# In the first block's mixers, ten of 25 input tiles and all twelve output tiles stay whole float32 and are multiplied in two passes; the other tiles are split as before

## The chip, the cores and the metric

The kernel runs on one core of a Trainium2 chip. A core has five engines that run side by side, each through its own list of instructions in order: TensorE (PE in the profile, its weight loads PEld), VectorE (DVE), ScalarE (ACT), GpSimd (POOL) and SyncE (SP), whose queue here issues nearly all loads from the chip's memory. The engines wait for one another by semaphores. The metric is the device time of one execution in microseconds (us).

## The reference

Two transformer-like blocks work one after the other on a sequence of 256 tokens of width 1024, in float32. Each block is a pair of token mixers followed by an expert layer (PEER) that scores 16,384 small experts. The change lies in the first block's mixers alone:

```
mod = (silu(c) @ w_ada + b_ada)              # six vectors of 1024: shifts, scales, gates
h = rmsnorm(x, norm_mix) * (1 + scale_m) + shift_m
proj = h @ w_in                              # 1024 -> 3088 columns
y_pool = pool_mixer(proj[:, :512])           # trailing means of 2, 4, 8, 16 tokens, then 128x128 per group
y_ssd = ssd_mixer(z, xbc, dt)                # causal convolution, SiLU, chunked state space, gate, rmsnorm
y = concat(y_pool, y_ssd) @ w_out            # 1536 -> 1024
x = x + gate_m * y
```

## The kernel before, in words

Everything is held transposed: a tile has 128 channels on the partitions and the 256 tokens in the free dimension. A weight tile is 128 by 8 by 128 float32 values (512 KB): the eight 128x128 blocks that make 128 output channels from 1024 inputs. The whole kernel consumes 645 such tiles in one fixed list (`self.items`), filled by `plan` and walked by `fetch_to` (L72: issue the load on SP), `high` (L79: ScalarE writes `whi`, the tile rounded to the matmul's reduced float32r type, L90), `low` (L93: VectorE writes `wlo = raw - whi`, L97) and `take` (L107), which prepares tiles two ahead of the product that it is called for and issues loads three tiles beyond that. `raw`, `whi` and `wlo` have three buffers each.

The activations are split in the same way into `hh` and `hl`. A product (`product_steps`, L119) then makes, for each of eight k, three float32r matmuls of 256 columns: `whi` by `hh` (L124), `whi` by `hl` (L125), `wlo` by `hh` (L126). Products land in PSUM buffers `mm`, of which there are three.

Nothing is scheduled by a planner: each engine's instructions stand in the order in which the Python code emits them. The first block's mixers (`mixer1`) run in this order:

- **The start** (L384 to L468). Sixteen rows of `w_ada` are reduced against `silu(c)` (`ada`, L306: a multiply with a running sum, L313 on VectorE; the first three on GpSimd and ScalarE). Along the way come the modulation (`g`, `mod`: L417, L418), the activations `h[k]` (ScalarE, for k of 6 and 7 VectorE, L426), `hh`, `hl` (`rest`, L431) and the products of the first two input tiles (`pair`), which run together, five of eight k inside the loop and three behind it.
- **The input tiles** (L716 on). 25 tiles in the order of `M1`: time steps, four tiles of B and C, eight of x, eight of z, four for pooling. After each product comes its evacuation (`evac`): a four-tap convolution (L357 on ScalarE, then three L359 on VectorE) and SiLU for the x, B and C tiles, a gate for z, sums over windows for pooling (L644 to L653). The list `steps` and the numbers in this loop place the state-space work beside it (`decays`, `outputs`), and from n = 5 on one `ada` row per tile. Work that has to wait a tile goes through the list `post`.
- **The outputs** (L745 on). Each output y is split into `yh` (ScalarE, L629, L665) and `yl` (VectorE, L630, L666). Eight tiles `w_outs` (1024 state-space channels) and four `w_outp` (512 pooling channels for two output tiles each; `both`, L752) follow: a pair, then in turns `out(f + 2)`, `residual(f)` and `both`. `residual` (L762) adds to x and prepares the next layer's split input `gh`, `gl`.
- **What follows.** The expert layer's first two products take `gh` and `gl` while the last residuals are made; then comes its norm, and the rest of the kernel, with 608 split tiles.

Of the kernel before, what the change touches and what calls it, by code (L numbers as in the profile page):

```python
# [18 lines left out]
T = 256  # L19
D = 1024  # L20
KT = 8
# [30 lines left out]
class Net:  # L52
# [16 lines left out]
    def plan(self, key, index, eng=None, spare=False):  # L69
        self.items.append([key, index, eng, None, spare])  # L70

    def fetch_to(self, n):  # L72
        while self.fetched < min(n, len(self.items)):
            it = self.items[self.fetched]
            it[3] = self.stream.tile([128, KT, 128], F32, name="raw", bufs=RAW)
            self.nc.sync.dma_start(it[3], self.a[it[0]][it[1]])
            self.fetched += 1

    def high(self, n):  # L79
# [4 lines left out]
        self.fetch_to(n + 1)  # L84
        if it[4]:
# [33 lines left out]
    def product_steps(self, ps, key, index, xh, xl, clear=True, prep=PREP):  # L119

        nc = self.nc
        hi, lo = self.take(key, index, prep)
# [11 lines left out]
    def proj(self, key, index, xh, xl):  # L134
# [229 lines left out]

    def plan_mixer1(self):
        for n, i in enumerate(self.M1):
            self.plan("w_in", i, eng=None)
        for f in range(0, 8, 2):
            self.plan("w_outs", f)
            self.plan("w_outs", f + 1)  # L370
            self.plan("w_outp", f // 2)

    def mixer1(self, constants):
        tc, nc, a = self.tc, self.nc, self.a
        with self.sbuf("m1") as m1, self.sbuf("w1", 2) as wk, self.psum("q1", 3) as self.pp, self.psum("p1", 3) as px:
            xs = m1.tile([128, 8, T], F32, name="xs")
            self.scratch_in(m1)
# [4 lines left out]
            with self.sbuf("early") as self.ap:  # L382
# [30 lines left out]
                h = {}  # L413

                def scaled(k):
# [4 lines left out]
                    h[k] = self.ap.tile([128, T], F32, name="nt4", bufs=4)  # L420
                    if k < 6:
                        nc.scalar.activation(self.hh[:, k], xs[:, k], AF.Identity, scale=g[:, k:k + 1],
                                             bias=m[:, k:k + 1])
                        nc.scalar.activation(h[k], xs[:, k], AF.Identity, scale=g[:, k:k + 1], bias=m[:, k:k + 1])
                    else:
                        nc.vector.tensor_scalar(h[k], xs[:, k], g[:, k:k + 1], m[:, k:k + 1], op0=ALU.mult,  # L426
                                                op1=ALU.add)
                        nc.scalar.copy(self.hh[:, k], h[k])

                def rest(k):  # L430
                    nc.vector.tensor_sub(self.hl[:, k], h.pop(k), self.hh[:, k].bitcast(F32))  # L431
# [3 lines left out]
                rests = {4: (0, 1), 5: (2, 3), 6: (4, 5), 7: (6, 7)}  # L435
# [1142 lines left out]
```

## Time and profile before

| | |
|---|---|
| median of 3 runs | 2187.42 us (2176.32 to 2188.99) |
| profiled execution | 2172.73 us, of which the span that the profile shows is 2170.9 us |
| first block's mixers in that span | 0 to about 199 us |
| busy over the span | TensorE 92%, VectorE 73%, ScalarE 51%, GpSimd 2% |
| load of one tile, from issue to landing | 3.2 to 4.6 us, median by kind |

In the profile, a row of the timeline has the start and the duration in us, the engine, the line of the program, the operation and its operands (out<-in); in brackets stands how long the engine had been idle and what ended that. The ends of matmuls are modelled and pipelined: one of 256 columns shows 0.28 us where the next starts 0.11 us after it, so TensorE's pace is read from starts, not from durations. The same holds, less so, for VectorE and ScalarE, whose next instruction starts a little before the end of the last.

### The profile page before, as it was taken

How to read it: one execution, taken by the hardware profiler on the slowest of the kernel's cores; microseconds unless marked ns; L12 is line 12 of the kernel's file. 1: busy time of each engine (PE TensorE's matmuls, PEld its weight loads, DVE VectorE, ACT ScalarE, POOL GpSimd, SP SyncE). 2: the span in 40 equal slices, each digit the busy share in tenths (PEclk: the TensorE clock that was granted, in tenths of full speed). 3: DMA queues.
4: the chain of work that ended last, by engine and by line, in shares of the span. 5: the costliest groups of instructions: out<-in, count | busy, mean ns of one | idle time of the engine just before them, and what ended most of it. 6: DMA issues, size and time to landing. Idle time of an engine off the chain costs nothing.

```text
span 2170.9 us, 41970 instructions
## 1 busy us (share of the span) xinstructions
PE 1987.4 (92%) x16976; PEld 1947.6 (90%) x16976; DVE 1581.9 (73%) x3061; ACT 1107.3 (51%) x1965; POOL 53.2 (2%) x52
## 2 busy tenths in 40 slices
PE   5888888877999999999999998987789999999998
PEld 4778888777999999999999998887779999999998
DVE  7998899788655556765688779998885555555555
ACT  4564444555544445444576554446554444444444
POOL 3021000000000000000000010000000000000000
PEclk9999999999999999999999999999999999999999
DMA  7755344322555555755545564443236555555553
GB/s 256 253 183 189 141 155 142 116 94 100 195 191 187 192 193 195 258 199 185 188 154 175 185 223 137 151 151 107 89 107 208 190 187 192 193 187 189 189 185 128
DMA packets 102723, 376.67 MB, mean 174 GB/s; under 512 B 11648, under 2 KB 12032, under 8 KB 101504
## 3 DMA queue, kind: packets, MB, share of 16 engines
q1 hardware_dynamic: 101520, 369.38, 49.1%
q0 software_dynamic: 576, 4.19, 0.5%
q8 instruction: 133, 2.18, 0.4%
q14 instruction: 62, 0.51, 0.1%
q10 hardware_dynamic: 432, 0.41, 0.1%
HBM read 370.80 MB, written 3.15 MB: 172 GB/s over the span
## 4 chain that ended last, share of the span: by engine, by line
PE 62%; DVE 27%; ACT 6%; issue 3%; DMA 1%; SPq 0%; DVEq 0%; ACTq 0%
PE acc L1341 11%; PE acc L1340 11%; PE acc L1342 11%; PE mm L126 9%; PE mm L125 9%; PE mm L124 9%; DVE wlo L97 8%; ACT whi L90 3%; DVE og L1236 2%; DVE aw L313 2%; DVE oh L1231 1%; DVE I L959 1%; DVE rep L965 1%; DVE X L1304 1%; DVE V L957 1%
## 5 line engine op out<-in xcount | busy, mean ns | idle before, releaser
L97 DVE TENSOR_TENSOR wlo<-raw,whi 128x1024 fp32r<-128x1024 f32 x642 | 786.3, 1226 | 330.8 <-ACT whi L90 329.1
L90 ACT CAST whi<-raw 128x1024 fp32r<-128x1024 f32 x642 | 672.2, 1048 | 187.7 <-PE acc L1341 135.5
L126 PE MATMUL mm<-hh,wlo 128*128 128x256 f32 x2376 | 671.0, 282 | 38.4 <-DVE wlo L97 38.2
L124 PE MATMUL mm<-hh,whi 128*128 128x256 f32 x2376 | 672.0, 283 | 11.5 <-ACT whi L90 8.9
L125 PE MATMUL mm<-hl,whi 128*128 128x256 f32 x2376 | 667.1, 281 | 10.5 <-DVE hl L431 6.5
L1340 PE MATMUL acc<-wh,whi 128*128 128x256 f32 x2048 | 573.6, 280 | 5.0 <-ACT wh L116 2.9
L1341 PE MATMUL acc<-wl,whi 128*128 128x256 f32 x2048 | 575.3, 281 | 0.2
L1342 PE MATMUL acc<-wh,wlo 128*128 128x256 f32 x2048 | 573.0, 280 | 0.0
L126 PEld LDWEIGHTS mm<-hh,wlo 128*128 128x128 f32 x2376 | 452.6, 190 | 48.3 <-DVE wlo L97 48.0
L124 PEld LDWEIGHTS mm<-hh,whi 128*128 128x128 f32 x2376 | 452.2, 190 | 15.5 <-ACT whi L90 10.1
L125 PEld LDWEIGHTS mm<-hl,whi 128*128 128x128 f32 x2376 | 453.6, 191 | 12.4 <-DVE hl L431 7.1
L1340 PEld LDWEIGHTS acc<-wh,whi 128*128 128x128 f32 x2048 | 386.4, 189 | 5.7 <-ACT wh L116 3.3
L1341 PEld LDWEIGHTS acc<-wl,whi 128*128 128x128 f32 x2048 | 385.8, 188 | 0.6 <-DVE wl L117 0.6
L1342 PEld LDWEIGHTS acc<-wh,wlo 128*128 128x128 f32 x2048 | 384.6, 188 | 0.0
L116 ACT CAST wh<-X 128x256 fp32r<-128x256 f32 x256 | 102.9, 402 | 184.4 <-PE acc L1342 184.4
L117 DVE TENSOR_TENSOR wl<-X,wh 128x256 fp32r<-128x256 f32 x256 | 107.9, 421 | 76.0 <-ACT wh L116 76.0
L1322 ACT ACTIVATE ge<-mm 128x256 f32<-128x256 f32 x128 | 49.0, 383 | 223.9 <-PE mm L126 223.9
L1196 DVE TENSOR_TENSOR X<-X,ge 128x256 f32<-128x256 f32 x144 | 60.5, 425 | 120.4 <-ACT ge L1322 119.9
L124 PE MATMUL acc<-hh,whi 128*128 128x256 f32 x480 | 145.5, 303 | 0.0
L1295 PEld LDWEIGHTS <-oh 128*128 128x128 f16 x1024 | 59.3, 97 | 84.9 <-DVE og L1236 70.8
L125 PE MATMUL acc<-hl,whi 128*128 128x256 f32 x480 | 134.7, 281 | 0.0
L126 PE MATMUL acc<-hh,wlo 128*128 128x256 f32 x480 | 134.2, 279 | 0.0
(345 smaller groups left out, 2066.3 us busy)
## 6 DMA issues: line engine op xcount, KB each, us to landing
raw<-in_down_dram SPq DMA_DIRECT2D x256, 512.0 KB, 3.2
raw<-in_up_dram SPq DMA_DIRECT2D x256, 512.0 KB, 3.9
raw<-in_w_in_dram SPq DMA_DIRECT2D x81, 512.0 KB, 3.3
aw<-in_w_ada_dram SPq DMA_DIRECT2D x48, 512.0 KB, 4.6
raw<-in_w_query_dram SPq DMA_DIRECT2D x32, 512.0 KB, 3.3
raw<-in_w_outs_dram SPq DMA_DIRECT2D x8, 512.0 KB, 3.8
raw<-in_w_out_dram SPq DMA_DIRECT2D x8, 512.0 KB, 3.9
raw<-in_w_outp_dram SPq DMA_DIRECT2D x4, 512.0 KB, 3.9
```

What stands on the lines that cost most here:

```text
L90: self.nc.scalar.copy(hi, it[3])
L97: (self.nc.gpsimd if it[2] == "pool" else self.nc.vector).tensor_sub(lo, raw, hi.bitcast(F32))
L116: self.nc.scalar.copy(hi, src)
L117: self.nc.vector.tensor_sub(lo, src, hi.bitcast(F32))
L124: nc.tensor.matmul(ps, hi[:, k], xh[:, k], start=k == 0 and clear, stop=False, skip_group_check=True)
L125: nc.tensor.matmul(ps, hi[:, k], xl[:, k], start=False, stop=False, skip_group_check=True)
L126: nc.tensor.matmul(ps, lo[:, k], xh[:, k], start=False, stop=k == KT - 1, skip_group_check=True)
L1196: nc.vector.tensor_mul(wf, wf, acts.pop(i))
L1295: nc.tensor.matmul(pg[:, j], o2[j], o1[:, j // 2, b, :, j % 2], start=b == 0, stop=b == 1, skip_group_check=True)
L1340: nc.tensor.matmul(o, hi[:, d], wh, start=i == 0 and d < 4, stop=False, skip_group_check=True)
L1341: nc.tensor.matmul(o, hi[:, d], wl, start=False, stop=False, skip_group_check=True)
L1342: nc.tensor.matmul(o, lo[:, d], wh, start=False, stop=i == NK - 1, skip_group_check=True)
```

## The change

The planner's items get a third kind. A tile planned with `whole="own"` is loaded into a pool of its own (`rawf`, three buffers, 12 KB per partition), one with `whole="shared"` into the ring `raw`; neither is split. Their products make one plain float32 matmul per k, which the hardware runs as two passes (two records in a trace, as the kernel's other float32 matmuls have). Whole are the input tiles 0, 1, 2, 4, 6, ... 16 of the 25 (`unsplit`) and all twelve output tiles. A whole tile's buffer is free when TensorE has made the product, a split one's when VectorE has written `wlo`.

For these products the activations must be there unsplit: `h` becomes eight tiles of a new array `ys`, of twelve tiles in all, which later takes the mixers' outputs in place of `yh` and `yl`. `hh` and `hl` are made from `h` behind the loop over the `ada` rows, `hh` by eight casts on ScalarE, `hl` by eight subtractions on VectorE. The removed instructions are 22 casts L90, 22 subtractions L97, 4 casts L665 and 12 `yl` (L630, L666); for `h` and `hh` ScalarE has 14 instructions before (L422, L424, L428) and 14 in the change; 528 split matmuls (22 times 24) become 176 float32 ones of two passes.

```diff
     def fetch_to(self, n):
         while self.fetched < min(n, len(self.items)):
             it = self.items[self.fetched]
-            it[3] = self.stream.tile([128, KT, 128], F32, name="raw", bufs=RAW)
+            if it[2] == "own":
+                it[3] = self.whole.tile([128, KT, 128], F32, name="rawf", bufs=RAW)
+            else:
+                it[3] = self.stream.tile([128, KT, 128], F32, name="raw", bufs=RAW)
...
         self.fetch_to(n + 1)
+        if it[2]:
+            it[3] = it[3],
+            return
...
-        hi, lo = self.take(key, index, prep)
+        w = self.take(key, index, prep)
+        if len(w) == 1:
+            for k in range(KT):
+                nc.tensor.matmul(ps, w[0][:, k], xh[:, k], start=k == 0 and clear, stop=k == KT - 1,
+                                 skip_group_check=True)
+                yield
+            return
+        hi, lo = w
...
+    def unsplit(self, n):
+
+        return n < 2 or n % 2 == 0 and n < 18
+
     def plan_mixer1(self):
         for n, i in enumerate(self.M1):
-            self.plan("w_in", i, eng=None)
+            self.plan("w_in", i, whole=self.unsplit(n) and "own")
         for f in range(0, 8, 2):
-            self.plan("w_outs", f)
-            self.plan("w_outs", f + 1)
-            self.plan("w_outp", f // 2)
+            self.plan("w_outs", f, whole="own")
+            self.plan("w_outs", f + 1, whole="shared")
+            self.plan("w_outp", f // 2, whole="own" if f % 4 else "shared")
...
-                    h[k] = self.ap.tile([128, T], F32, name="nt4", bufs=4)
                     if k < 6:
-                        nc.scalar.activation(self.hh[:, k], xs[:, k], AF.Identity, scale=g[:, k:k + 1],
-                                             bias=m[:, k:k + 1])
-                        nc.scalar.activation(h[k], xs[:, k], AF.Identity, scale=g[:, k:k + 1], bias=m[:, k:k + 1])
+                        nc.scalar.activation(h[:, k], xs[:, k], AF.Identity, scale=g[:, k:k + 1], bias=m[:, k:k + 1])
...
-                    for f in rests.get(k, ()):
-                        rest(f)
...
                 self.prep_to(3)
                 for _ in both:
                     pass
+                for k in range(KT):
+                    nc.scalar.copy(self.hh[:, k], h[:, k])
+                for k in range(KT):
+                    nc.vector.tensor_sub(self.hl[:, k], h[:, k], self.hh[:, k].bitcast(F32))
...
-                        nc.scalar.mul(yh[:, 4 + p], y, gn)
-                        post.append(lambda: nc.vector.scalar_tensor_tensor(
-                            yl[:, 4 + p], y, gn, yh[:, 4 + p].bitcast(F32), op0=ALU.mult, op1=ALU.subtract))
+                        nc.scalar.mul(ys[:, 4 + p], y, self.v("ssd_norm", p))
...
-                ps = self.proj("w_in", i, self.hh, self.hl)
+                ps = self.proj("w_in", i, *([h] if self.unsplit(n) else [self.hh, self.hl]))
...
-                        nc.tensor.matmul(o, hi[:, kk], yh[:, k], start=False, stop=False, skip_group_check=True)
-                        nc.tensor.matmul(o, hi[:, kk], yl[:, k], start=False, stop=False, skip_group_check=True)
-                        nc.tensor.matmul(o, lo[:, kk], yh[:, k], start=False, stop=k == 3, skip_group_check=True)
+                        nc.tensor.matmul(ps[f][:, 1], w[:, 4 * b + k], ys[:, k], start=False, stop=k == 3,
+                                         skip_group_check=True)
```

VectorE at the end of the start, where h[6] and h[7] are made (`nt`, in the change `ys`). Before:

```order
L313 SCALAR_TENSOR_TENSOR aw,mod<-aw,crow 128x1024 x2
L417 TENSOR_TENSOR mod<-mod,vecs 128x1
L418 SCALAR_TENSOR_TENSOR g<-mod,b_145,vecs 128x1
L426 TENSOR_SCALAR nt_294<-xs,g,mod 128x256
L431 TENSOR_TENSOR hl<-nt_280,hh 128x256
L431 TENSOR_TENSOR hl<-nt_285,hh 128x256
L313 SCALAR_TENSOR_TENSOR aw,mod<-aw,crow 128x1024 x2
L97 TENSOR_TENSOR wlo<-raw,whi 128x1024
L417 TENSOR_TENSOR mod<-mod,vecs 128x1
L418 SCALAR_TENSOR_TENSOR g<-mod,b_145,vecs 128x1
L426 TENSOR_SCALAR nt_339<-xs,g,mod 128x256
```

The same place in the change:

```order
L326 SCALAR_TENSOR_TENSOR aw,mod<-aw,crow 128x1024 x2
L436 TENSOR_TENSOR mod<-mod,vecs 128x1
L437 SCALAR_TENSOR_TENSOR g<-mod,b_149,vecs 128x1
L442 TENSOR_SCALAR ys<-xs,g,mod 128x256
L326 SCALAR_TENSOR_TENSOR aw,mod<-aw,crow 128x1024 x2
L436 TENSOR_TENSOR mod<-mod,vecs 128x1
L437 SCALAR_TENSOR_TENSOR g<-mod,b_149,vecs 128x1
L442 TENSOR_SCALAR ys<-xs,g,mod 128x256
L481 TENSOR_TENSOR hl<-ys,hh 128x256 x8
```

The subtraction for a weight tile and the `hl` pairs between the `ada` rows are gone, and all eight `hl` stand in one row behind the last h.

VectorE at the last two input tiles (n = 23 and 24). Before, from the third pooling output (`po`) on:

```order
L661 TENSOR_SCALAR po<-aux,vecs 128x256
L313 SCALAR_TENSOR_TENSOR aw,mod<-aw,crow 128x1024
L97 TENSOR_TENSOR wlo<-raw,whi 128x1024
L630 SCALAR_TENSOR_TENSOR yl<-yo,vecs,yh 128x256
L622 SCALAR_TENSOR_TENSOR yo<-xs,vecs,aux 128x256
L623 SCALAR_TENSOR_TENSOR yo<-yo,zs 128x256
L648 TENSOR_TENSOR ps_1662<-pu 128x271
L651 SCALAR_TENSOR_TENSOR pmx<-ps_1662,pu 128x256
L652 TENSOR_TENSOR pmx<-ps_1662,cnt 128x16
L653 TENSOR_TENSOR pmx<-pmx,pu 128x16
L661 TENSOR_SCALAR po<-aux,vecs 128x256
L97 TENSOR_TENSOR wlo<-raw,whi 128x1024
```

In the change:

```order
L668 TENSOR_SCALAR ys<-aux,vecs 128x256
L326 SCALAR_TENSOR_TENSOR aw,mod<-aw,crow 128x1024
L633 SCALAR_TENSOR_TENSOR yo<-xs,vecs,aux 128x256
L634 SCALAR_TENSOR_TENSOR yo<-yo,zs 128x256
L656 TENSOR_TENSOR ps_1437<-pu 128x271
L659 SCALAR_TENSOR_TENSOR pmx<-ps_1437,pu 128x256
L660 TENSOR_TENSOR pmx<-ps_1437,cnt 128x16
L661 TENSOR_TENSOR pmx<-pmx,pu 128x16
L668 TENSOR_SCALAR ys<-aux,vecs 128x256 x3
```

No `wlo` and no `yl` stands between the last state-space output (`yo`), the last pooling input (`pmx`) and the pooling outputs.

SP, from the load of input tile 2 to the small constants (a wait on a DMAHW semaphore is for an earlier load, DVE and PE for those engines). Before:

```order
L76 DMA raw<-in_w_in_dram 128x1024 [waits DMAHW6_49]
L76 DMA raw<-in_w_in_dram 128x1024 [waits DMAHW7_49,DVE_49]
L76 DMA raw<-in_w_in_dram 128x1024 [waits DMAHW2_49,DMAHW0_49,DVE_49]
L76 DMA raw<-in_w_in_dram 128x1024 [waits DMAHW6_49,DMAHW1_49,DVE_49]
L472 DMA U<-in_cst_dram 128x128
```

In the change:

```order
L79 DMA rawf<-in_w_in_dram 128x1024 [waits DMAHW6_49]
L79 DMA raw<-in_w_in_dram 128x1024 [waits DMAHW7_49]
L79 DMA rawf<-in_w_in_dram 128x1024 [waits DMAHW0_49,PE_49]
L79 DMA raw<-in_w_in_dram 128x1024 [waits DMAHW1_49]
L485 DMA U<-in_cst_dram 128x128 [waits DMAHW2_49]
```

Tile 4, the third row, now waits for TensorE's product of tile 0, and what stands behind it on SP's queue waits with it; tiles 3 and 5 wait for no engine.

## Rows read from the trace of the kernel before

**Rows 1.** The page: busy time over the span, and VectorE's tenths in 40 slices.
```profile
PE 1987.4 (92%) x16976; PEld 1947.6 (90%) x16976; DVE 1581.9 (73%) x3061; ACT 1107.3 (51%) x1965; POOL 53.2 (2%) x52
...
DVE  7998899788655556765688779998885555555555
```

**Rows 2.** Stretches: us, then PE, PEld, DVE, ACT, POOL busy, PEclk, DMA, GB/s.
```profile
46.00:97.00 51.00, 44.51 (x357) 41.69 (x357) 48.28 (x102) 25.42 (x47) 0.00 (x0) 1.00 0.70 244
97.00:135.00 38.00, 35.82 (x280) 32.01 (x280) 37.83 (x68) 28.74 (x69) 2.32 (x4) 0.96 0.65 235
135.00:165.50 30.50, 21.34 (x159) 19.76 (x159) 28.70 (x52) 13.46 (x29) 10.19 (x9) 0.89 0.40 142
165.50:198.70 33.20, 29.01 (x243) 28.05 (x243) 30.07 (x63) 14.87 (x24) 5.54 (x4) 1.00 0.51 179
```

**Rows 3.** The chain of waits from 46 to 165 us, shares by engine and line.
```profile
by line: DVE wlo L97 20.0%; DVE aw L313 14.5%; DVE cva L359 11.6%; issue 6.5%; PE mm L125 4.7%; PE mm L126 4.6%; PE mm L124 4.5%; DVE ps L648 3.8%; DVE yl L630 3.5%; DVE mt L600 3.2%; DVE xs L679 2.6%; DVE pmx L652 2.2%; DVE zs L689 1.5%; D
```

**Rows 4.** A group of VectorE's, 29 to 166 us: busy us, mean ns | idle before.
```profile
L97 DVE TENSOR_TENSOR wlo<-raw,whi 128x1024 fp32r<-128x1024 f32 x28 | 35.1, 1256 | 0.0
```

**Rows 5.** VectorE's timeline: the start of an instruction to the start of the next.
```profile
126.45 1.22 DVE L97 TENSOR_TENSOR wlo<-raw,whi 128x1024 fp32r<-128x1024 f32 x1
127.59 0.47 DVE L630 SCALAR_TENSOR_TENSOR yl<-yo,vecs,yh 128x256 fp32r<-128x256 f32 x1
127.98 0.41 DVE L689 SCALAR_TENSOR_TENSOR zs<-th,mm 128x256 f32<-128x256 f32 x1
```

**Rows 6.** TensorE's timeline: a split product's k steps, and float32 matmuls of 256 columns.
```profile
147.03 0.28 PE L124 MATMUL mm<-hh,whi 128*128 128x256 f32 x1
...
147.37 0.28 PE L124 MATMUL mm<-hh,whi 128*128 128x256 f32 x1
...
162.28 1.02 PE L659 MATMUL aux<-pmx,pw 128*128 128x256 f32 x4
```

**Rows 7.** All of that line's records: ns min/median/max.
```profile
L659 PE MATMUL aux<-pmx,pw x8: 378/379/484, 145.8 to 162.9; 128*128 128x256 f32 x8
```

**Rows 8.** VectorE's timeline at the end of the start.
```profile
37.17 0.75 DVE L431 TENSOR_TENSOR hl<-nt,hh 128x256 fp32r<-128x256 f32 x2
...
45.39 0.41 DVE L426 TENSOR_SCALAR nt<-xs,g,mod 128x256 f32<-128x256 f32 x1
...
48.34 1.52 DVE L359 SCALAR_TENSOR_TENSOR cva<-mm,hcw,cva 128x255 f32<-128x255 f32 x3 [1.32 <-ACT cva L357]
```

**Rows 9.** ScalarE's timeline: the state-space decays, one group per input tile.
```profile
130.58 1.14 ACT L592 ACTIVATE mt<-aux,asT 128x128 f32<-128x128 f32 x4 [0.51 <-PE aux L588]
...
135.26 1.14 ACT L592 ACTIVATE mt<-aux,asT 128x128 f32<-128x128 f32 x4 [0.53 <-PE aux L588]
```

**Rows 10.** TensorE's waits, 46 to 215 us: total, times, longest us.
```profile
PE aux L587 <- DVE xdt L559: 3.1, 2, 2.2
```

**Rows 11.** GpSimd's timeline: an `ada` row at n = 22.
```profile
139.55 3.32 POOL L310 TENSOR_TENSOR aw<-aw,crow 128x1024 f32<-128x1024 f32 x1
```

**Rows 12.** VectorE's timeline in the same stretch, and at the end of the input tiles.
```profile
140.55 2.60 DVE L630 SCALAR_TENSOR_TENSOR yl<-yo,vecs,yh 128x256 fp32r<-128x256 f32 x1
...
157.71 0.42 DVE L623 SCALAR_TENSOR_TENSOR yo<-yo,zs 128x256 f32<-128x256 f32 x1
...
165.57 0.16 DVE L165 TENSOR_SCALAR re<-sm 128x2 f32<-128x2 f32 x1 [0.27 <-PE sm L224]
```

**Rows 13.** TensorE's timeline: waits in the output pair and behind it.
```profile
156.95 0.58 PE L126 MATMUL mm<-yh,wlo 128*128 128x256 f32 x1 [6.04 <-DVE wlo L97]
...
160.31 0.41 PE L126 MATMUL mm<-yh,wlo 128*128 128x256 f32 x1
160.53 0.32 PE L124 MATMUL mm<-yh,whi 128*128 128x256 f32 x1
...
206.11 0.61 PE L224 MATMUL sm<-ones,ns 128*128 128x1 f32 x4 [1.63 <-POOL ns L219]
```

**Rows 14.** DMA issues: KB each, median us from issue to landing.
```profile
raw<-in_w_outs_dram SPq DMA_DIRECT2D x8, 512.0 KB, 3.8
```

More of the change, by code (lines that the diff above doesn't have):

```diff
@@ L66, in psum, with plan @@
         return self.tc.tile_pool(name=name, bufs=bufs, space=PSUM, reuse_waits="tile")
-    def plan(self, key, index, eng=None, spare=False):
-        self.items.append([key, index, eng, None, spare])
+    def plan(self, key, index, whole=False, spare=False):
+        self.items.append([key, index, whole, None, spare])
     def fetch_to(self, n):
@@ L363 @@
     M1 = [24, 20, 21, 22, 23] + list(range(12, 20)) + list(range(4, 12)) + [3, 2, 1, 0]
+    def unsplit(self, n):
+        return n < 2 or n % 2 == 0 and n < 18
     def plan_mixer1(self):
         for n, i in enumerate(self.M1):
[L367 removed]
+            self.plan("w_in", i, whole=self.unsplit(n) and "own")
         for f in range(0, 8, 2):
[L369 to L371 removed]
+            self.plan("w_outs", f, whole="own")
+            self.plan("w_outs", f + 1, whole="shared")
+            self.plan("w_outp", f // 2, whole="own" if f % 4 else "shared")
     def mixer1(self, constants):
         tc, nc, a = self.tc, self.nc, self.a
[L375 removed]
+        with self.sbuf("wf") as self.whole, self.sbuf("m1") as m1, self.sbuf("w1", 2) as wk, self.psum("q1", 3) as self.pp, self.psum("p1", 3) as px:
             xs = m1.tile([128, 8, T], F32, name="xs")
+            ys = m1.tile([128, 12, T], F32, name="ys")
+            h = ys[:, 4:]
             self.scratch_in(m1)
@@ L438, in mixer1 @@
                 first = [self.pp.tile([128, T], F32, name="mm") for _ in range(2)]
-                both = self.pair(first, [("w_in", i) for i in self.M1[:2]], self.hh, self.hl, prep=1)
+                both = self.pair(first, [("w_in", i) for i in self.M1[:2]], h, None, prep=1)
                 for f in range(KT):
@@ L489, in mixer1 @@
             nc.vector.tensor_scalar(aneg, aneg, -1.0, None, op0=ALU.mult)
-            yh = m1.tile([128, 12, T], F32R, name="yh")
-            yl = m1.tile([128, 12, T], F32R, name="yl")
             bc = m1.tile([128, 4, T], F32, name="bc")
@@ L749, in out @@
                 q = ps[f] = self.pp.tile([128, 2, T], F32, name="mm")
-                self.product(q[:, 0], "w_outs", f, yh[:, 4:], yl[:, 4:])
+                self.product(q[:, 0], "w_outs", f, ys[:, 4:], None)
             def both(j):
-                hi, lo = self.take("w_outp", j)
+                w, = self.take("w_outp", j)
                 for b in range(2):
@@ L795, in mixer1 @@
                 ps[f] = self.pp.tile([128, 2, T], F32, name="mm")
-            two = self.pair([ps[0][:, 0], ps[1][:, 0]], [("w_outs", 0), ("w_outs", 1)], yh[:, 4:], yl[:, 4:])
+            two = self.pair([ps[0][:, 0], ps[1][:, 0]], [("w_outs", 0), ("w_outs", 1)], ys[:, 4:], None)
             for _ in range(KT - 2):
@@ L1047, in plan_peer @@
             elif st[0] == "U":
[L1048 removed]
+                self.plan(up, st[1])
                 early = max(early - 1, 0)
```

27 lines of the change are left out of this document (7 added, 20 removed).

## Prediction

> **What bounds the kernel now.** The page first: TensorE is busy for 92% of the span, VectorE for 73%, but the average hides the stage that the change touches: in the first four of the 40 slices VectorE stands at 7 to 9 tenths and above [rows 1]. So I cut the mixers into stretches [rows 2]. From 46 to 135 us VectorE is busy for 86.1 of 89 us and TensorE for 80.3; from 135 to 165.5 VectorE for 28.7 of 30.5, TensorE for 21.3; then, in the output products, both are near 90%. The chain of waits says which of the two sets the pace: from 46 to 165 us the largest share is the subtraction that splits a weight tile (`wlo`, 20%), the three matmul lines of the split products have 14% together [rows 3]. VectorE sets the pace in most of the mixers, and the largest single thing on it, 28 subtractions of 1.26 us [rows 4], is what the change takes from.
>
> One stretch is different. While the state-space work runs (n = 13 to 21), ScalarE's decays wait for TensorE's `aux` in every step and come every 4.68 us [rows 9]. By the pace below, TensorE has there a split product (2.72), six float32 matmuls of 128 columns in two passes and four float32r ones of 256 columns (an estimate of 1.73, from half a float32 pass and a third of a k step for each): 4.45 of the 4.68. TensorE is the bound there, with VectorE close behind.
>
> **What a product costs.** A split product starts a k step every 0.34 us (147.03 to 147.37), so 2.72 us for eight. The four records of two float32 matmuls of 256 columns, back to back, last 1.02 us, one record 0.379, so a pass follows the last after (1.02 - 0.38)/3 = 0.213 us [rows 6, 7]. A whole product is 16 passes: 3.41 us, 0.69 more than a split one. That holds for full clock; at half clock it is twice that.
>
> What VectorE gives back I count by pitch, from start to start: 1.14 us for a `wlo`, 0.39 for a `yl` [rows 5], 0.37 for an `hl` [rows 8]. One `yl` lasted 2.60 us [rows 12]; it ran while GpSimd multiplied an `ada` row for 3.32 us and ended with it [rows 11]. I save 0.39 there, not 2.6, for the GpSimd multiply stays and the instructions that move up (two inputs in SBUF among them) meet it in its place. The Trainium skill (SBUF — State Buffer, Who interferes with whom) says that a VectorE instruction with two SBUF inputs and a GpSimd one that reads SBUF exclude each other for a whole instruction; the trace agrees with the 2.60. By that rule too the wait moves; a reader who takes the row alone would put the sum 2.2 us lower.
>
> **The change, part by part,** in us against the profiled execution.
>
> *Start, to the first convolution at 48.34.* Ahead of the last `nt` at 45.39 go three `wlo` (3.42) and six `hl` (2.24): h[7] is done 5.66 earlier, at 45.80 - 5.66 = 40.14. Behind it now stand eight `hl` (2.96) and four small instructions (0.4): VectorE is free at 43.5. TensorE has then 0.85 (half clock 1.7) of the pair left after h[7], and ScalarE's part of the convolution 0.5, so 42.4 at the latest; it is hidden. The eight casts for `hh` are on ScalarE, six of them ahead of h[7], hidden. On SP the load of tile 4 now waits for the pair (42.4 at the latest) with tile 5 and the constants behind it; it lands 3.8 later [rows 14], tile 4 is due at 48.6 and the `wlo` of tile 5 at 47.8: hidden, though by 2 us only, and if tile 5 comes late, its split waits, and tile 5's product behind it. The convolution starts at 43.5: **-4.8**. Bounds: -3.5 (the `ada` rows' own loads may hold them up, which no row shows) and -5.7.
>
> *Tiles 2 to 12, VectorE's stretch.* The `wlo` of tiles 4, 6, 8, 10, 12 and 14 go: -6.84. TensorE has 3.41 and 2.72 in turn, 6.1 for two tiles; VectorE had 8.5 (51 us for twelve tiles [rows 2]) and has 7.4, so it stays the bound in the mean. The exception is the beginning, where TensorE is not yet ahead: tile 3 needs its `wlo`, which comes behind the first convolution (43.5 + 1.4 + 1.14 = 46.1), so it ends about 48.6 and tile 4 at 52.0; VectorE, ready then, waits for ScalarE's part of the convolution: I give back 0.8. ScalarE's casts that go count nothing; they lay beside VectorE's work. **-6.0**. Bounds: -4 (one more such wait per two whole tiles), -6.84.
>
> *Tiles 13 to 21, TensorE's stretch.* Tiles 14 and 16 are whole: +1.4. The `wlo` of tile 16 and three `yl` (2.3) go from VectorE, which does not bound there; the shorter of TensorE's two waits for VectorE's `xdt` (3.1 - 2.2 = 0.9 [rows 10]) goes: **+0.5**. Bounds: +1.4, and -2.3 if VectorE is the bound after all.
>
> *Pooling tiles and the output pair, VectorE's stretch again.* Up to the last `yo` at 157.71 go two `wlo` (2.28) and three `yl` (1.17); VectorE was 0.4 late at the first pooling tile: -3.85. Behind it the last pooling input is ready at 156.0 instead of 3.85 later. TensorE ran dry at 150.91 (156.95 - 6.04); two `wlo` earlier the pair starts, at about 148.5, and has its first six k (24 passes, 5.1 us) behind it by 153.6. TensorE waits for that input (2.4 us, where before it waited 6.04 for a `wlo` and then ran 3.6 us at half clock, matmuls of 0.41 [rows 13]), and has then 0.43 for a pooling matmul, 1.71 for two k of two tiles, 0.5 for the sums. So VectorE's `re` starts at 158.65, not at 165.57 [rows 12]: **-6.9**. Bounds: -5, -7.
>
> *Ten whole output tiles.* 34.1 us, and 0.45 for `spread`: 34.55, with VectorE no longer splitting beside it and TensorE's waits for residuals gone. Before, this took 33.2 with those waits [rows 2]: **+1.35**. Bounds: 0, +3 (if the waits stay). The loads: a whole tile's buffer is free only after its product, but the next tile of that slot is needed at least three products (10.2 us) later, against 3.8 us for a load [rows 14]: hidden.
>
> *To the next layer's sums at 206.11 [rows 13].* From the end of the output products (198.7, where I ended the stretch) to them a `wlo` and three residuals stood on VectorE, then a square and GpSimd's sum: 7.4 us. The `wlo` (1.14) and the residual before the last two (1.3) now come under the last output products, and so does the 0.4 of a `gl`: 4.6: **-2.8**. Bounds: 0, -2.8.
>
> Everything behind is unchanged and shifts. Sum: -4.8 - 6.0 + 0.5 - 6.9 + 1.35 - 2.8 = **-18.6**; the profiled execution of 2172.7 would become 2154. It is the fastest of the four times shown; its median of three is 2187.4, and from there the sum gives 2169, which is my number. With all bounds at one end the gain is 9, at the other 25.
>
> **Rivals.** *All of VectorE's work counts.* If VectorE bounds n = 13 to 21 too (it is busy there for 37.8 of 38.0 us [rows 2], which speaks for it; the decays' wait for TensorE speaks against), the third term is -2.3 and the 0.8 is not given back: -22.2, so 2165 from the median.
>
> *TensorE takes over early.* Whole products are longer, PSUM lets TensorE run ahead by three tiles only, and a wait of about 1.4 us at each of the six whole tiles from 4 to 14 would eat 8: a gain near 10, 2177. For it: at tile 4 it happens by my own sum. Against: VectorE needs 7.4 us for two tiles, TensorE 6.1.
>
> *TensorE at half clock in the output tiles: slower.* Twelve whole products take 41 us at full clock and 82 at half. If more than 45% of that work ran at half clock, the gain is gone; throughout, the kernel is 22 slower, 2210. For it: the pair started so before [rows 13]. Against: it did so after 6.04 us without work, and its wait is now 2.4 us, between dense products. The Trainium skill (TensorE: Matmul & The Clock Gate, Part 1) has half clock as the state that an idle TensorE falls back to and steady work ends; the trace agrees, with 0.41 us at 160.31 and 0.32 at 160.53.
>
> *The change doing nothing* is out: 22 subtractions leave an engine that is busy for 97% of the input tiles' time.
>
> **Numbers.** Forecast (a gain of 12 to 21) 0.56; all of VectorE's work counts (21 to 26) 0.27; TensorE takes over (3 to 12) 0.11; slower 0.06. 1% is 21.9 us, about what a measurement of this kernel can tell from no change. The forecast lies 3 us short of it, and the runs before spread over 13 us, so some of the forecast's weight (0.05) goes over that line; of the slower case a third stays within it. Faster by over 1%: 0.32; within 1%: 0.64; slower by over 1%: 0.04. The range runs from the largest gain against the profiled time (2172.7 - 26 = 2147) to a gain of 4 against the median (2183).
>
> **What would show it.** The first convolution on VectorE at 43 to 44 us. Records of float32 passes 0.213 apart in the whole products. The decays 4.4 to 4.7 apart from n = 17 on, and about 10 us earlier than before at n = 20. VectorE idle for some us between 95 and 125, waiting for TensorE. TensorE's wait ahead of the last pooling matmul 2 to 3 us in place of 6, and output products back to back, 3.41 each. The sums at 206.11 near 187.5. I am wrong if whole products wait for their loads, if passes are further apart than 0.213, or if TensorE is seen at half clock behind the pair.

## The result, and the profile after

The median is 2162.53 us (2151.22 to 2165.38, four runs) against 2183.78 for the kernel before (2176.32 to 2188.99, four runs): 21.3 us less, a ratio of 0.9896 with a 95% interval of 0.9846 to 0.9945. Timed again later, on one chip with two of the experiments, the same kernel stood at 0.990 (0.9876 to 0.9924). I had put it at 18.6 us less, 2169 from the median then known (2187.42; the fourth time brought it to 2183.78).

The profiled execution after the change (2165.38, span 2163.6) is only 7.3 us shorter than the one before. In the mixers alone it is 19.2 us ahead: the next layer's sums begin at 186.92, not at 206.11 [rows 13]. The missing 11.9 us lie behind that mark, in code that the change does not touch (more below). So I compare by marks in the mixers, which agree between two executions of the change to 0.25 us.

| from mark to mark | before | after | forecast | measured |
|---|---|---|---|---|
| span's start to the first convolution | 48.34 | 44.26 | -4.8 | -4.08 |
| to the `ada` row of n = 12 | 46.57 | 41.04 | -6.0 | -5.53 |
| to the `ada` row of n = 21 | 42.82 | 41.40 | +0.5 | -1.42 |
| to `re` | 27.84 | 21.00 | -6.9 | -6.84 |
| to the expert layer's first product | 33.15 | 34.68 | +1.35 | +1.53 |
| to its sums | 7.39 | 4.54 | -2.8 | -2.85 |
| all | 206.11 | 186.92 | -18.6 | -19.19 |

The page after, busy time and VectorE's slices, to be set beside [rows 1]: the average hardly tells of the change (VectorE 73% before, 72% now); its third and fourth slices go from 9 and 8 to 8 and 7.

```profile
PE 2006.1 (93%) x16800; PEld 1959.0 (91%) x16800; DVE 1552.5 (72%) x3027; ACT 1083.9 (50%) x1939; POOL 51.7 (2%) x52
...
DVE  7987998787555556755687769997875555555555
```

The stretches tell it. They end at the marks that answer to those of [rows 2]; the columns are the same.

```profile
42.00:87.40 45.40, 44.15 (x282) 40.02 (x281) 42.14 (x98) 18.52 (x38) 0.00 (x0) 1.00 0.82 295
87.40:124.10 36.70, 36.30 (x280) 31.41 (x278) 36.53 (x65) 28.76 (x69) 2.73 (x4) 1.00 0.73 256
124.10:147.70 23.60, 20.55 (x143) 18.43 (x143) 21.22 (x40) 8.39 (x21) 10.03 (x9) 1.00 0.39 144
147.70:182.38 34.68, 34.68 (x162) 30.52 (x162) 23.61 (x62) 7.46 (x17) 5.83 (x5) 1.00 0.54 194
```

In the first stretch TensorE is now as busy as VectorE (97% and 93%, before 87% and 95%); in the second both are at 99%. In the output products TensorE is never idle, and VectorE's work has fallen from 30.1 to 23.6 us. The granted clock is 1.00 in all four, where it was 0.89 in the third before.

TensorE's timeline after the change: the last pooling input, two whole output products, the expert layer's first product and its sums.

```profile
144.93 0.67 PE L667 MATMUL aux<-pmx,pw 128*128 128x256 f32 x2 [1.53 <-DVE pmx L661]
...
151.49 3.62 PE L131 MATMUL mm<-ys,rawf 128*128 128x256 f32 x16
154.95 3.62 PE L131 MATMUL mm<-ys,raw 128*128 128x256 f32 x16
...
182.38 0.47 PE L137 MATMUL acc<-gh,whi 128*128 128x258 f32 x1
...
186.92 0.50 PE L237 MATMUL sm<-ones,ns 128*128 128x1 f32 x4
```

TensorE's wait ahead of the last pooling matmul is 1.53 us where it waited 6.04 for a `wlo` [rows 13]; a whole product takes 3.46 from start to start, 16 passes of 0.216.

### The profile page after: what moved, and what is told of

Its sections match the earlier page's. It is cut to its first block, busy times and chain, and to the rows that moved or that the text cites. A ratio compares the mean times of both kernels' runs of the same rounds, so it can differ in the third digit from the quotient of the medians.

```text
span 2163.6 us, 41532 instructions
## 1 busy us (share of the span) xinstructions
PE 2006.1 (93%) x16800; PEld 1959.0 (91%) x16800; DVE 1552.5 (72%) x3027; ACT 1083.9 (50%) x1939; POOL 51.7 (2%) x52
## 4 chain that ended last, share of the span: by engine, by line
PE 64%; DVE 25%; ACT 6%; issue 3%; DMA 1%; SPq 0%; DVEq 0%; ACTq 0%
PE acc L1339 11%; PE acc L1341 11%; PE acc L1340 11%; PE mm L139 9%; PE mm L138 9%; PE mm L137 9%; DVE wlo L103 7%; ACT whi L96 3%; DVE og L1235 2%; DVE aw L326 2%; DVE oh L1230 1%; DVE I L958 1%; DVE rep L964 1%; DVE X L1303 1%; PE mm L131 1%
## 5 line engine op out<-in xcount | busy, mean ns | idle before, releaser
L103 DVE TENSOR_TENSOR wlo<-raw,whi 128x1024 fp32r<-128x1024 f32 x620 | 758.6, 1224 | 327.6 <-ACT whi L96 325.8
L96 ACT CAST whi<-raw 128x1024 fp32r<-128x1024 f32 x620 | 648.8, 1047 | 179.9 <-PE acc L1340 137.3
L139 PE MATMUL mm<-hh,wlo 128*128 128x256 f32 x2296 | 650.1, 283 | 35.9 <-DVE wlo L103 35.8
L137 PE MATMUL mm<-hh,whi 128*128 128x256 f32 x2296 | 650.7, 283 | 2.3 <-ACT X L1132 1.4
L138 PE MATMUL mm<-hl,whi 128*128 128x256 f32 x2296 | 646.4, 282 | 4.1 <-DVE hl L261 1.9
L139 PEld LDWEIGHTS mm<-hh,wlo 128*128 128x128 f32 x2296 | 438.5, 191 | 44.5 <-DVE wlo L103 44.1
L138 PEld LDWEIGHTS mm<-hl,whi 128*128 128x128 f32 x2296 | 435.6, 190 | 5.5 <-DVE hl L261 2.7
L137 PEld LDWEIGHTS mm<-hh,whi 128*128 128x128 f32 x2296 | 434.3, 189 | 5.2 <-ACT X L1132 1.6
```

The lines of the kernel that those rows point to most:

```text
L96: self.nc.scalar.copy(hi, it[3])
L103: self.nc.vector.tensor_sub(lo, raw, hi.bitcast(F32))
L137: nc.tensor.matmul(ps, hi[:, k], xh[:, k], start=k == 0 and clear, stop=False, skip_group_check=True)
L138: nc.tensor.matmul(ps, hi[:, k], xl[:, k], start=False, stop=False, skip_group_check=True)
L139: nc.tensor.matmul(ps, lo[:, k], xh[:, k], start=False, stop=k == KT - 1, skip_group_check=True)
```

## The experiments

Two names for the theories: by the **ledger**, each part of the change is worth what the engine that sets the pace of its stretch gains or loses, and the parts add up. The rivals say that another engine sets that pace, or that the parts hang together. All marks are in us from the span's start, in each kernel's profiled execution.

### The halves alone

For the inputs alone, `yh`, `yl` and the split output products come back (`h` then has a place of its own, the room for it and for the whole tiles is given back ahead of the outputs, and `yl` is allotted behind the start):

```diff
-            self.plan("w_outs", f, whole="own")
-            self.plan("w_outs", f + 1, whole="shared")
-            self.plan("w_outp", f // 2, whole="own" if f % 4 else "shared")
+            self.plan("w_outs", f)
+            self.plan("w_outs", f + 1)
+            self.plan("w_outp", f // 2)
```

> Inputs alone: the ten input tiles are whole as in the change, the twelve output tiles are split as before, so the yh and yl instructions are back. Marks, before / change: first convolution on VectorE 48.34 / 44.26; ada row of n = 12 94.91 / 85.30; ada row of n = 21 137.73 / 126.70; re 165.57 / 147.70; the next layer's sums 206.11 / 186.92. The parts add up (my ledger): the input half is worth 10 us at the sums, so 196.3, with the marks up to n = 12 as in the change, and from n = 21 on the distances of before (27.8 to re, 40.5 from re to the sums). Three yl come back before n = 21: that row at 127.9 if VectorE sets the pace there, at 126.7 if TensorE does. Rival, that the two halves help each other (the whole output tiles gain only because VectorE is ahead): the sums later than 199.

For the outputs alone, the start is that of the kernel before, and no input tile is whole:

```diff
-        return n < 2 or n % 2 == 0 and n < 18
+        return False
```

> Outputs alone: all input tiles split and the start as before, the twelve output tiles whole. Ledger: marks up to n = 20 as before (first convolution 48.3, n = 12 94.9), n = 21 at 136.6 to 137.7, then the change's distances: 21.0 to re (158), 34.7 for the output products and 4.5 to the sums: 197 to 198, a gain of 8 to 9. Rival, the whole output tiles gain only because VectorE is ahead: the sums later than 201. Rival, TensorE at half clock in whole products: passes 0.43 apart instead of 0.216 and the sums later than 206.

The marks, inputs alone and outputs alone: first convolution 44.28 and 48.53; row of n = 12 85.42 and 95.09; row of n = 21 127.13 and 137.67; `re` 154.71 and 158.98. The sums, from TensorE's timeline of the inputs alone:

```profile
195.45 0.61 PE L237 MATMUL sm<-ones,ns 128*128 128x1 f32 x4 [1.63 <-POOL ns L232]
```

and of the outputs alone:

```profile
198.19 0.50 PE L237 MATMUL sm<-ones,ns 128*128 128x1 f32 x4
```

The halves give 10.66 and 7.92 us, 18.58 together, against 19.19 for the whole change. So the parts add up, to 0.6 us. (With the inputs alone the row of n = 21 fell between the two places that I had given.) With the outputs alone three `yl` (1.17 us) are gone ahead of the row of n = 21. This kernel is 0.19 behind the one before from its first convolution on. ScalarE's decays, which wait for TensorE, are 0.19 behind at every step (the last at 135.45, before at 135.26): to TensorE the three `yl` were worth nothing. VectorE's own row (137.67, before 137.73) came only 0.25 earlier by that reckoning, for three of its multiplications lasted 0.54 longer, beside GpSimd's sums of squares (a `ce` of 0.95 and one of 0.96 us, an `mt` of 1.22, against 0.41 and 0.68); before it was 0.75 in all, in two.

### Which engine sets the pace of n = 13 to 21

Tiles 14 and 16 split again:

```diff
-        return n < 2 or n % 2 == 0 and n < 18
+        return n < 2 or n % 2 == 0 and n < 14
```

> The change, with tiles 14 and 16 split again: two subtractions (2.3 us) back on VectorE, 1.4 us less on TensorE. If TensorE sets the pace from n = 13 on, as my third term had it: n = 21 at 125.3 and the sums at 185.5. If VectorE sets it: n = 21 at 129.0 and the sums at 189.2. What I now think from the decays (16 to 23 of them stand 10.8 to 10.9 us earlier than before at every step, 4.67 apart in both, so all of the 1.4 us came ahead of n = 16): VectorE sets the pace up to n = 16, TensorE behind it, and the cost of the two whole products lay in a wait; so VectorE's result, 1.5 to 2.3 later, all of it ahead of the decays of n = 16, which come at 101.6 to 102.4 instead of 100.12.

Tiles 18 and 20 whole too (`h` has eight tiles of its own, since `ys` is written from n = 18 on):

```diff
-        return n < 2 or n % 2 == 0 and n < 18
+        return n < 2 or n % 2 == 0 and n < 22
```

> The change, with input tiles 18 and 20 whole too (twelve whole input tiles; h has room of its own for that): two subtractions (2.3 us) less on VectorE, 1.5 us more on TensorE, in the stretch n = 17 to 21 alone. If TensorE sets the pace there (decays 4.67 apart before and after, whatever VectorE had to do): the steps with a whole product take 5.4 instead of 4.67, n = 21 comes at 127.9 to 128.3 instead of 126.70, the sums 1.2 to 1.6 later, near 188.3. If VectorE sets the pace there too (busy in all of it): n = 21 at 124.4 and the sums at 184.7.

ScalarE's timeline, one group of decays per input tile. After the change:

```profile
88.40 1.14 ACT L603 ACTIVATE mt<-aux,asT 128x128 f32<-128x128 f32 x4
91.65 1.14 ACT L603 ACTIVATE mt<-aux,asT 128x128 f32<-128x128 f32 x4
100.12 1.15 ACT L603 ACTIVATE mt<-aux,asT 128x128 f32<-128x128 f32 x4 [1.81 <-PE aux L599]
104.80 1.15 ACT L603 ACTIVATE mt<-aux,asT 128x128 f32<-128x128 f32 x4 [0.51 <-PE aux L599]
110.32 1.14 ACT L603 ACTIVATE mt<-aux,asT 128x128 f32<-128x128 f32 x4 [0.89 <-PE aux L599]
115.00 1.14 ACT L603 ACTIVATE mt<-aux,asT 128x128 f32<-128x128 f32 x4 [0.51 <-PE aux L599]
119.67 1.14 ACT L603 ACTIVATE mt<-aux,asT 128x128 f32<-128x128 f32 x4 [0.51 <-PE aux L599]
124.34 1.14 ACT L603 ACTIVATE mt<-aux,asT 128x128 f32<-128x128 f32 x4 [0.52 <-PE aux L599]
```

The same before, the first six groups (the last two are [rows 9]):

```profile
98.00 1.14 ACT L592 ACTIVATE mt<-aux,asT 128x128 f32<-128x128 f32 x4
102.39 1.14 ACT L592 ACTIVATE mt<-aux,asT 128x128 f32<-128x128 f32 x4
110.87 1.14 ACT L592 ACTIVATE mt<-aux,asT 128x128 f32<-128x128 f32 x4 [1.51 <-PE aux L588]
115.63 1.14 ACT L592 ACTIVATE mt<-aux,asT 128x128 f32<-128x128 f32 x4 [0.52 <-PE aux L588]
121.24 1.14 ACT L592 ACTIVATE mt<-aux,asT 128x128 f32<-128x128 f32 x4 [0.90 <-PE aux L588]
125.91 1.14 ACT L592 ACTIVATE mt<-aux,asT 128x128 f32<-128x128 f32 x4 [0.51 <-PE aux L588]
```

With tiles 14 and 16 split:

```profile
102.57 1.14 ACT L603 ACTIVATE mt<-aux,asT 128x128 f32<-128x128 f32 x4 [1.67 <-PE aux L599]
```

With tiles 18 and 20 whole too:

```profile
115.54 1.14 ACT L604 ACTIVATE mt<-aux,asT 128x128 f32<-128x128 f32 x4 [0.75 <-PE aux L600]
120.92 1.14 ACT L604 ACTIVATE mt<-aux,asT 128x128 f32<-128x128 f32 x4 [1.35 <-PE aux L600]
125.59 1.14 ACT L604 ACTIVATE mt<-aux,asT 128x128 f32<-128x128 f32 x4 [0.53 <-PE aux L600]
```

What TensorE waited for in n = 13 to 16, from its timelines before, after the change, and with tiles 14 and 16 split:

```profile
98.26 0.38 PE L587 MATMUL aux<-ah,identr 16*128 16x256 f32 x1 [2.20 <-DVE xdt L559]
```

```profile
99.36 0.38 PE L598 MATMUL aux<-ah,identr 16*128 16x256 f32 x1 [0.40 <-DVE xdt L570]
```

```profile
89.97 0.38 PE L598 MATMUL aux<-ah,identr 16*128 16x256 f32 x1 [1.39 <-DVE xdt L570]
...
101.81 0.38 PE L598 MATMUL aux<-ah,identr 16*128 16x256 f32 x1 [1.10 <-DVE xdt L570]
```

Read the leads over the kernel before: 9.60 at the first group, 10.74 at the second, 10.75 at the third, 10.83 at the fourth, 10.91 or 10.92 at the last four. The 1.14 us between the first and the second are one `wlo`, at VectorE's pitch; behind that no step is more than 0.1 shorter than before. With tiles 14 and 16 split, the group of 100.12 comes at 102.57, 2.45 later (I had put 1.5 to 2.3), and the sums at 189.36: two `wlo` cost VectorE's price. The two shorter products give TensorE nothing but longer waits for VectorE's `xdt`, 2.49 in place of 0.40. With 18 and 20 whole, two steps take 0.7 longer (one 5.38 instead of 4.67), the row of n = 21 comes at 127.81 and the sums at 188.01, 1.1 later. VectorE gained at first (its rows of n = 16 and 18 came 1.0 and 1.9 us earlier than in the change), then waited and had lost it by n = 20: there two `wlo` less give nothing in the end, and the longer products cost. So VectorE sets the pace up to about n = 16 and TensorE behind it, as I had expected of both by then.

### The start

VectorE's and ScalarE's small instructions go ahead of the `hl`:

```diff
-                for k in range(KT):
-                    nc.vector.tensor_sub(self.hl[:, k], h[:, k], self.hh[:, k].bitcast(F32))
...
             nc.vector.tensor_scalar(aneg, aneg, -1.0, None, op0=ALU.mult)
+            for k in range(KT):
+                nc.vector.tensor_sub(self.hl[:, k], h[:, k], self.hh[:, k].bitcast(F32))
```

> The change, with VectorE's four small instructions behind the start (identr, hcw, vecs, aneg) moved ahead of the eight hl. In the change ScalarE waited 2.40 us for vecs, and its part of the first convolution stood behind that; VectorE then waited 0.90 for it. If that queue is what my first term missed (4.1 instead of 4.8): the first convolution at 43.3 to 43.5 instead of 44.26, the sums near 186.1. If the pair on TensorE is the cause: 44.26 as before. If the load of tile 5, which ScalarE waits for until 47.33, takes it back: the convolution at 43.4 and the row of n = 5 at 59.2 as in the change.

What it was to mend, in the profile after: ScalarE's timeline, then VectorE's.

```profile
43.30 0.21 ACT L501 ACTIVATE vecs<-vecs 128x8 f32<-128x8 f32 x1 [2.40 <-DVE vecs L500]
43.42 0.34 ACT L518 COPY dtr<-mm 16x256 f32<-16x256 f32 x1
43.67 0.55 ACT L370 ACTIVATE cva<-mm,hcw 128x256 f32<-128x256 f32 x1
```

```profile
40.26 2.77 DVE L481 TENSOR_TENSOR hl<-ys,hh 128x256 fp32r<-128x256 f32 x8
...
44.26 1.52 DVE L372 SCALAR_TENSOR_TENSOR cva<-mm,hcw,cva 128x255 f32<-128x255 f32 x3 [0.90 <-ACT cva L370]
```

ScalarE stood 2.40 us in a wait for `vecs`, which VectorE reached behind the eight `hl`; ScalarE's part of the convolution was queued behind that wait. In the experiment the first convolution began at 43.77, without a wait, 0.5 earlier (I had put 43.3 to 43.5; VectorE now waits 0.35 for ScalarE ahead of `aneg`), but the row of n = 5 stood at 59.37 (59.20 in the change) and the sums at 186.82. TensorE's timeline in the change, then TensorE's and VectorE's in this kernel, show what took it back:

```profile
40.40 4.58 PE L131 MATMUL mm<-ys,rawf 128*128 128x256 f32 x20 [0.23 <-DVE ys L442]
```

```profile
40.48 6.27 PE L131 MATMUL mm<-ys,rawf 128*128 128x256 f32 x20 [1.93 <-DVE ys L442]
```

```profile
47.38 1.52 DVE L372 SCALAR_TENSOR_TENSOR cva<-mm,hcw,cva 128x255 f32<-128x255 f32 x3 [0.96 <-ACT cva L370]
```

The same 20 passes (the end of the pair and tile 2) took 4.58 us in the change, after a wait of 0.23. Here they took 1.7 longer, at a mean granted clock of 0.73, and VectorE waited 0.96 at the second convolution for the product that came late. In a second execution of the change (below) they took 6.27 as well, and its sums stood at 186.96: the slow passes cost the change itself nothing, they only take the edit's gain. Moved alone, with the clock as it fell, the edit gave nothing; it is tried again below.

### VectorE and GpSimd

The two `ada` rows of n = 22 and 24, which GpSimd multiplies, go to VectorE:

```diff
-                    self.ada(lates.pop(0), n in (22, 24))
+                    self.ada(lates.pop(0))
```

> The change, with the two ada rows of n = 22 and n = 24, which GpSimd multiplies and ScalarE sums, on VectorE like the others. That adds 2 x 1.14 us of work to VectorE. In the change three VectorE instructions last long while those rows are on GpSimd: a wlo 1.74, a yo 2.10, an aw 3.26, together 4.3 over their usual 1.22, 0.42 and 1.22. If VectorE and GpSimd hold each other up there: the three are back at their usual lengths, VectorE is 2.0 ahead at the end, TensorE's waits for mt and pmx (1.5 each) shrink, and re comes 1 to 2 us earlier, at 145.7 to 146.7, the sums near 185.5. If those lengths have another cause: re 2.3 later, near 150, the sums near 189.2.

GpSimd's timeline after the change, and VectorE's beside it:

```profile
128.51 3.31 POOL L323 TENSOR_TENSOR aw<-aw,crow 128x1024 f32<-128x1024 f32 x1
...
138.78 2.35 POOL L323 TENSOR_TENSOR aw<-aw,crow 128x1024 f32<-128x1024 f32 x1 [0.85 <-DMA aw<-in_w_ada_dram]
```

```profile
130.01 2.10 DVE L634 SCALAR_TENSOR_TENSOR yo<-yo,zs 128x256 f32<-128x256 f32 x1
...
138.96 3.26 DVE L326 SCALAR_TENSOR_TENSOR aw<-aw,crow 128x1024 f32<-128x1024 f32 x1
```

VectorE in the experiment, the same two instructions, a row that came from GpSimd, and `re`:

```profile
130.16 0.42 DVE L634 SCALAR_TENSOR_TENSOR yo<-yo,zs 128x256 f32<-128x256 f32 x1
...
138.71 1.21 DVE L326 SCALAR_TENSOR_TENSOR aw<-aw,crow 128x1024 f32<-128x1024 f32 x1
...
142.87 1.22 DVE L326 SCALAR_TENSOR_TENSOR aw<-aw,crow 128x1024 f32<-128x1024 f32 x1
145.41 0.16 DVE L178 TENSOR_SCALAR re<-sm 128x2 f32<-128x2 f32 x1 [0.41 <-PE sm L237]
```

Both are back at their usual length; the `wlo` of 1.74 that I had put down to the same cause kept its length; in the change a sum of squares on GpSimd (1.63 us from 126.87) lies beside it, not one of these rows. `re` comes 2.29 earlier and the sums 2.30 (184.62), a little more than I expected: 3.7 us of waiting go, one row of 1.14 is added ahead of the last pooling input, and the other (142.87) stands behind it, where VectorE has time. What the change saved in `yl` by the row of 2.60 [rows 12] was thus only moved to other instructions. The Trainium skill (SBUF — State Buffer, Who interferes with whom) says that a VectorE instruction with two SBUF inputs contends with a GpSimd instruction that reads SBUF, for a port that is locked for one of them; 2.10 against 0.42 and 3.26 against 1.21 agree.

### The last input tile, and the output tiles

Tile 24 whole too:

```diff
-        return n < 2 or n % 2 == 0 and n < 18
+        return n < 2 or n % 2 == 0 and n < 18 or n == 24
```

> The change, with input tile 24 whole too (h has room of its own): one subtraction less on VectorE, 1.74 long in the change, 1.14 by its pitch, behind the row of n = 21; 0.74 more on TensorE. VectorE sets the pace from there to re, with TensorE 1.5 behind nothing at pmx. By VectorE alone 1.1 less; TensorE, which then comes to the last pooling matmul at 143.95 instead of 143.2, allows 1.0: re at 146.6 to 146.8, the sums at 185.9. If TensorE sets the pace: re 0.7 later, 148.4, the sums at 187.7.

`re` came at 146.77 and the sums at 185.98: 0.93 and 0.94 earlier, as expected.

Three `w_outp` tiles split again (the odd `w_outs` tiles behind the first then go through `rawf`):

```diff
-            self.plan("w_outs", f + 1, whole="shared")
-            self.plan("w_outp", f // 2, whole="own" if f % 4 else "shared")
+            self.plan("w_outs", f + 1, whole="own" if f else "shared")
+            self.plan("w_outp", f // 2, whole=not f and "shared")
...
                 residual(f)
+                if f == 0:
+                    for k in range(4):
+                        nc.scalar.copy(yh[:, k], ys[:, k])
+                    for k in range(4):
+                        nc.vector.tensor_sub(yl[:, k], ys[:, k], yh[:, k].bitcast(F32))
```

> The change, with the last three of the four w_outp tiles split again, and four casts and four subtractions (1.5 us on VectorE) for the pooling outputs' yh and yl behind the first residual. By my theory TensorE sets the pace in the output products now (3.46 each, VectorE busy for 22 of 34 us there): three products of 2.72 instead of 3.46 give 2.2, the acc products begin at 180.2 instead of 182.38, the sums near 184.7. If VectorE is what the whole output tiles wait for (its residuals hold PSUM buffers): no gain, or 1 to 2 later.

The expert layer's products began at 182.00, 0.4 earlier instead of 2.2, and the sums at 188.71, 1.8 later. VectorE's timeline of this kernel, then TensorE's:

```profile
152.99 1.23 DVE L103 TENSOR_TENSOR wlo<-raw,whi 128x1024 fp32r<-128x1024 f32 x1 [2.33 <-ACT whi L96]
...
172.78 1.23 DVE L103 TENSOR_TENSOR wlo<-raw,whi 128x1024 fp32r<-128x1024 f32 x1 [1.35 <-ACT whi L96]
```

```profile
155.57 3.72 PE L131 MATMUL mm<-ys,rawf 128*128 128x256 f32 x16 [0.52 <-DVE x L775]
...
175.71 3.72 PE L131 MATMUL mm<-ys,rawf 128*128 128x256 f32 x16 [0.48 <-DVE x L775]
```

ScalarE's timeline, the cast ahead of the second of these subtractions:

```profile
171.70 1.04 ACT L96 CAST whi<-raw 128x1024 fp32r<-128x1024 f32 x1 [6.42 <-DMA raw<-in_w_outp_dram]
```

In the change VectorE has 11 us to spare there, but here a residual stands in its queue behind a `wlo` that waits for ScalarE's cast; the residual comes late, and TensorE waits for the PSUM buffer that it frees. The last residual began 2.8 us later than in the change (185.94 and 183.19), and the sums come behind it. My theory that TensorE alone sets the pace there was too simple: the whole tiles also take those waits out of VectorE's queue. But the cast itself waited 6.42 us for its load, which was issued at 166.38 where the change issues that tile's load at 162.05. Whether the other buffers of this edit made that load late, and how much of the loss is the split's own, this run does not show.

### Timed again, with the two edits that promised something

> The change itself again, for its time on the chip of the next two. The mixers' part is the same in every run to 0.2 us, so the sums again at 186.9; the rest of the program, the same code in all, took between 1958 and 1977 us in the profiled executions so far. If that spread is the runs' and not the kernel's, this profile's rest lies anywhere in it, not at the upper end again. The ratio to the kernel before: 0.991 by my ledger (19.2 of 2180).

> The kernel without ada rows on GpSimd again, timed: 21.5 us below the kernel before by its marks (206.11 - 184.62), a ratio of 0.990, 2.3 us below the change, which five rounds will hardly tell apart.

> No ada rows on GpSimd, and the four small instructions ahead of the eight hl. With the first alone the sums stood at 184.6. If TensorE's half clock took back what the second gave (20 passes took 6.27 us where they took 4.58 elsewhere), and TensorE runs them at full clock this time: the row of n = 5 at 58.8 and the sums at 184.1. At half clock again, or if something else holds the row of n = 5: 59.3 and 184.6. Ratio to the kernel before 0.990.

Six runs each, against eleven of the kernel before (median 2178.51, 2169.36 to 2186.99):

| kernel | sums at | median us | ratio to before, 95% interval |
|---|---|---|---|
| the change | 186.96 | 2159.76 (2154.26 to 2163.0) | 0.990 (0.9876 to 0.9924) |
| no rows on GpSimd | 184.45 | 2154.86 (2146.83 to 2162.95) | 0.9878 (0.985 to 0.9906) |
| that, and the small instructions first | 184.13 | 2160.41 (2156.18 to 2162.84) | 0.9904 (0.988 to 0.9927) |

In the third kernel the 20 passes took 4.58 us after a wait of 1.38, the row of n = 5 stood at 58.87 (59.16 in the second) and the sums 0.32 earlier; so the load of tile 5 does not hold that row at 59.2. The last h happened to come 0.29 later in this execution (the 20 passes began at 40.64, in the second kernel at 40.35), so from there on the edit gave 0.6. By the marks both beat the change, by 2.5 and 2.8 us; by their times none of the three can be told from the others.

## Why the prediction was right, and the step that failed

The ledger held: each term but one is within 0.8 us of its mark, and the sum within 0.6. That the sum is closer than its terms is luck: the first two were 1.2 us too large together and the third 1.9 too small. (My bounds on the side of the small gain add up to 8.1, not to 9.) That VectorE sets the pace where I put it is shown for tile 14, whose `wlo` stands ahead of the row of n = 12 (86.61 with it, 85.30 without), and for tile 24; for tiles 4 to 12 it is read from the table and was not tested. TensorE's price for a whole product, 16 passes, is shown by the starts 3.46 apart and by the steps that tiles 18 and 20 made 0.7 longer.

The step that failed is the third: "*Tiles 13 to 21, TensorE's stretch*", +0.5 forecast and -1.42 measured. I read the pace of n = 17 to 21 off two rows of decays 4.68 apart [rows 9] and laid it over n = 13 to 16 as well, where VectorE set it. So I charged 1.4 us for tiles 14 and 16 on an engine that had slack there, and gave nothing for the `wlo` of tile 16, which brought its whole 1.14. The slack was in [rows 10]: of TensorE's two waits for `xdt` I let the shorter one go, 0.9 us; in the change both together fell from 3.1 to 0.4. There was more of it in the granted clock of 0.96 [rows 2]: before, TensorE ran the product behind the wait of 2.20 at half clock (0.50 from 100 to 102 us, matmuls 0.21 apart), and still waited 0.92 behind it; in the change the clock is 1.00 there. Three groups of decays more (98.00, 102.39, 110.87) would have shown where the pace of 4.67 begins. The rival that all of VectorE's work counts was wrong as well, behind n = 16: with the outputs alone, three `yl` less moved the decays by nothing. One sign that I had named did not show: VectorE never waits between 95 and 125 us. Part of what it had to spare went into longer instructions beside GpSimd's sums of squares (1.65 us in three of them, before 0.75 in two).

The first term was 0.7 too large. I had ScalarE's part of the convolution ready at 42.4; it was queued behind ScalarE's own wait for `vecs`, which stood behind the eight `hl`. Moving those instructions brought the mark forward by 0.5 us, and it reached the sums where TensorE kept its clock.

The third rival, half clock in the output tiles, did not come: passes 0.216 apart and a granted clock of 1.00. My argument against it was weaker than I took it for, though. I set a wait of 2.4 us against the 6.04 behind which TensorE ran at half clock; in the same trace it did so behind a wait of 2.20 (98.26) too. The second, TensorE taking over early, holds for tiles 3 to 5 only: TensorE's wait for the `wlo` of tile 3 was 1.2 us, VectorE's waits for ScalarE's part of the convolutions 1.1 us, and the term came out at -5.53 instead of -6.0. Of the pooling stretch, the tail and the output products each was right to 0.2 us, and by the mechanism: from the row of n = 21 on, the last pooling matmul came after 18.23 us, where I had its input ready after 18.27. TensorE's wait for it, 2 to 3 us in my forecast, was 1.53, since another pooling matmul (at 142.80) stood in the gap.

## What to carry to other kernels

Give each stretch of a stage its own pace-setter, and look for the mark where it changes hands: a subtraction taken from VectorE was worth its whole pitch on one side of n = 16 and nothing on the other. An instruction that waits also holds what is queued behind it on its engine, so work put on an engine with time to spare can still make the bound engine wait.

## What the runs showed of the hardware that I had not expected

The unchanged rest of the program, from the sums to the end of the span, took 1964.8 us in the profiled execution before, 1976.7 in that after, 1971.0 in the change's second profile, and from 1958.6 to 1974.7 in the others. Part of it is TensorE's pace in dense stretches. Two stretches of 100 us in the same code, before and after (columns as in [rows 2]):

```profile
1806.11:1906.11 100.00, 100.00 (x867) 100.00 (x866) 57.86 (x73) 48.20 (x73) 0.00 (x0) 1.00 0.55 190
```

```profile
1786.92:1886.92 100.00, 100.00 (x851) 100.00 (x851) 56.58 (x71) 47.96 (x72) 0.00 (x0) 1.00 0.54 185
```

TensorE is busy throughout at a granted clock of 1.00 in both, yet makes 867 matmuls in the one and 851 in the other, 1.9% fewer. In the execution with the small instructions alone moved, both appear: 40 weight tiles take 111.1 us in an earlier dense stretch and 113.1 in a later one. The execution before has both too (111.07 from 603 us on, 113.07 from 931, 111.07 from 1702), and the one with three `w_outp` tiles split has a third (108.80 from 922). So the pace does not go with the kernel; what sets it stays open.

At the end of the start TensorE waits for the last h and then runs 20 passes. After waits of 0.23 to 1.38 us they took 4.58 us in all four executions; after 1.81 to 1.94 they took 4.58 in two and 6.27 in five. The granted clock is 1.00 over the 4.58 us of the change; over the 6.27 us with the small instructions alone moved it is 0.73 (0.50 from 42 to 44 us; columns as in [rows 2]):

```profile
40.48:46.75 6.27, 6.27 (x21) 4.97 (x22) 5.52 (x16) 2.46 (x6) 0.00 (x0) 0.73 0.71 250
```

The Trainium skill (TensorE: Matmul & The Clock Gate, Part 1) has an idle TensorE fall back to half clock; the 6.27 agrees, and the two of 4.58 show that such a wait does not always bring it.
